# Last two output chunks merged into one, and DMA prices by row length in the planner of a hybrid decoder layer

## The chip, the core and the metric

The program runs on one core of one Trainium2 chip. The time is device microseconds of one execution; three executions of the kernel before gave 2155.23, 2158.32 and 2154.3 us, with a median of 2155.23 us. A separate, profiled execution took 2156.18 us, of which 2154.4 us is the span from its first to its last instruction. All durations below come from that execution.

## The reference, cut to what matters

One decoder layer is applied to 2048 prompt tokens and to 8 single decode tokens, all in float32 with width 1024. In the part that the change touches, the final RMSNorm divides each token's row by its root mean square and writes it out:

```python
x = x + jnp.concatenate([attn_out, conv_out, ssm_out], -1) @ w_out
hf = rmsnorm(x, norm_ffn_g)
x = x + (jax.nn.silu(hf @ w_ff_gate) * (hf @ w_ff_up)) @ w_ff_down
...
y_prompt = rmsnorm(xp, norm_final_g)     # (1, 2048, 1024)
y_sample = rmsnorm(xs, norm_final_g)     # (8, 1, 1024)
```

Before that lie the input projection, a sliding-window attention, a convolution and a state-space model (the first 650 us or so), and the output projection.

## The kernel before, in words

All 2056 tokens (2048 and then the 8) pass through one core. A float32 product is made of three passes of TensorE over a high and a low part of each operand, so each weight block that is loaded (`wraw`, `xraw`) is converted by ScalarE into its high part (`whl<-wraw`) and by VectorE or GpSimd into its low part before TensorE can use it. The first stages work in four quarters of 512 tokens. The gate and up products of the feed-forward part use a scheme with seven block products instead of eight: weight sums (`sw`) are formed on VectorE, kept in a scratch tensor (`sum`), and read back for later groups. The feed-forward part runs over three groups of tokens (g = 0, 1, 2; 688, 684 and 684 tokens), each group over 11 pairs of hidden blocks: gate and up products go to PSUM banks of the tag `mm` (three banks) or `tr` (two), the down products to `sc` (three), and VectorE adds the down products to an accumulator `xa`, which is eight tiles of features by tokens.

**The planner.** Nothing in the program is ordered by hand: class `Flow` (lines 45 to 174) simulates the kernel while it is being built. Each task is a generator that yields the engine it wants next, the buffers (tags) that it needs and the events it waits for. `Flow.run` (line 110) takes, again and again, the task that can begin first by the simulated clocks; among those of the same engine that begin within that engine's `SLACK` (TensorE 100 ns, VectorE 200, ScalarE 0, SyncE 50) it takes the one of the best priority. The order so found is each engine's instruction order on the chip, and each engine runs its queue in order: an instruction that waits holds everything behind it on that engine. All transfers are issued by SyncE through `Flow.dma` (line 163). It keeps one simulated clock, `DMA`, for all of them: a transfer begins when the one before it has ended, takes its bytes at 360 bytes per ns, or at 180 if a row is under 512 bytes, and counts as landed 2000 ns after its end. "Row" is the last dimension of the access, in bytes: 512 for a block of 128 columns of `w_ff_gate`, 2048 for `sum`, 4096 for `w_ff_down`, 1368 or 1376 for `hraw`.

Every instruction of the compute engines is emitted in one helper, so the profile puts them all on line 226; DMA issues are on line 164.

**The end of the kernel.** `final` (line 2187) handles one chunk of tokens. It waits for the down products of its tokens, takes two PSUM banks, transposes the eight `xa` tiles into them (four in each), has ScalarE square and sum each bank (`junkf`), VectorE add the two sums, ScalarE take the root (`stf`), VectorE invert it and scale the two halves by it and by the norm's weights (two instructions, 1.41 us in all), and SyncE write the chunk out. Group 2 has seven chunks: five of 128 tokens, one of the last 36 prompt tokens, and one of the 8 decode tokens. Their bank tags are written out in the tuple in `final`: `tr mm tr mm sc tr mm`. Chunk buffers for the result alternate between the tags `tx` and `whl`.

Of the kernel before, what the change touches and what calls it, by code (L numbers as in the profile page):

```python
# [19 lines left out]
T = 2048  # L20
NS = 8
# [31 lines left out]
class Flow:  # L53
# [89 lines left out]
    def rel(self, tag):  # L143
        self.free[tag].append(self.cur["fin"])
        self.free[tag].sort()
# [17 lines left out]
    def dma(self, out, in_):  # L163
        r = self.nc.sync.dma_start(out, in_)
        c = self.cur
        if c is not None:
            size, run = 4.0, 4.0 * min(in_.shape[-1], out.shape[-1])
            for d in in_.shape:
                size *= d
            start = max(self.clock["SP"], c["begin"])  # L170
            self.clock["SP"] = start + (650.0 if in_.shape[0] in (8, 64) else 475.0)
            self.clock["DMA"] = max(self.clock["DMA"], start + 1125.0) + size / 360.0 * (1.0 if run >= 512 else 2.0)
            c["fin"] = max(c["fin"], self.clock["DMA"] + 2000)
        return r

# [55 lines left out]
def hybrid_step(  # L231
# [13 lines left out]
    V, S = Engine(fl, "DVE", nc.vector), Engine(fl, "ACT", nc.scalar)  # L245
    G, E = Engine(fl, "POOL", nc.gpsimd), Engine(fl, "PE", nc.tensor)
    dma, rel = fl.dma, fl.rel
    ctx.enter_context(tc.manual_schedule())

# [89 lines left out]
    def load_unit(u, prio, pool=None, tag="whl", bufs=WB, after=0.0, keep=False, low="POOL"):  # L339
# [6 lines left out]
        def again():  # L346
            yield "SP", tag, kept_ev[u.key], *order
            taken.hit(0.0)
            hl = (pool or wpool).tile([P, 2, 1024], F32R, tag=tag, name=tag, bufs=bufs)
            dma(hl.bitcast(F32), kept[u.key])  # L350
            u.hl = hl.rearrange("p h (k c) -> p h k c", c=P)
            u.ready.hit(fl.now())
# [5 lines left out]
        def one():  # L358
            yield ("SP", "wraw", *([wturn] if wturn else []))
            wtaken.hit(0.0)  # L360
            raw = wpool.tile([P, 1024], F32, tag="wraw", name="wraw", bufs=2)
            u.load(raw)
            yield "ACT", tag, *order
            taken.hit(0.0)
            hl = (pool or wpool).tile([P, 2, 1024], F32R, tag=tag, name=tag, bufs=bufs)
            S.activation(hl[:, 0, :], raw, AF.Copy)
            yield low
            (G if low == "POOL" else V).tensor_tensor(hl[:, 1, :], raw, hl[:, 0, :].bitcast(F32), op=OP.subtract)
            rel("wraw")
            u.hl = hl.rearrange("p h (k c) -> p h k c", c=P)  # L370
            u.ready.hit(fl.now())
            if keep:
                yield "SP"
                dma(kept[u.key], hl.bitcast(F32))
                kept_ev[u.key].hit(fl.now())
# [1341 lines left out]
    G0 = [0, 688, 1372]  # L1717
# [39 lines left out]
    def tx_tile():  # L1757
        return bpool.tile([P, 1376], F32, tag="tx", name="tx", bufs=2)
# [179 lines left out]
    down_ev = {(g, j, a): Ev(KT // 2) for g in range(3) for j in range(2) for a in range(2)}  # L1938
    gu_ev = {g: Ev() for g in range(3)}
# [154 lines left out]
    b = "B22"  # L2094
# [85 lines left out]
    chunks = {}  # L2180
    for g in range(3):
        end = min(2 * GN[g], T - G0[g])
        chunks[g] = [(y_prompt[0, G0[g] + c:G0[g] + min(c + P, end), :], c, min(P, end - c)) for c in range(0, end, P)]
    chunks[2].append((y_sample[:, 0, :], T - G0[2], NS))
    fin_left = {g: len(chunks[g]) for g in range(3)}

    def final(g, i, dst, c0, n):

        bank = ("tr", "mm", "tr", "mm", "sc", "tr", "mm")[i] if g == 2 else "tr"
        st = fpool.tile([P, 4], F32, tag="stf", name="stf", bufs=4)  # L2190
        ev = Ev(2)
        for a in range(2):
            need = [down_ev[g, j, a] for j in range(2) if j * GN[g] < c0 + n and c0 < (j + 1) * GN[g]]
            if a == 0:
                yield ("PE", bank, bank, *need) if bank == "tr" else ("PE", bank, bank, gu_ev[2], *need)
                pts = [{"mm": ps_mm, "sc": ps_sc, "tr": ps_tr}[bank]() for _ in range(2)]
            else:
                yield ("PE", *need)
            pt = pts[a]
            for k in range(4):  # L2200
                E.transpose(pt[:n, k * P:(k + 1) * P], X[g, 4 * a + k][:, c0:c0 + n], ident)

            def square(a=a, pt=pt):
                yield "ACT"
                S.activation(junk[:n], pt[:n, :], AF.Square, accum_out=st[:n, a:a + 1])
                ev.hit(fl.now())
            fl.add(square(), 4)
        fin_left[g] -= 1
        if fin_left[g] == 0:
            for _ in range(KT):  # L2210
                rel("xa")
        tag = "whl" if g == 2 and i % 2 else "tx"
        yield ("DVE", ev, tag, gu_ev[2]) if tag == "whl" else ("DVE", ev, tag)
        if tag == "tx":
            y = tx_tile()[:, :D]
        else:
            y = wpool.tile([P, 2, D], F32R, tag="whl", name="y3", bufs=WB).bitcast(F32)[:, 0]
        V.tensor_tensor(st[:n, 0:1], st[:n, 0:1], st[:n, 1:2], op=OP.add)
        yield "ACT"
        S.activation(st[:n, 1:2], st[:n, 0:1], AF.Sqrt, scale=1.0 / D, bias=eps[:n])  # L2220
        yield "DVE"
        V.reciprocal(st[:n, 2:3], st[:n, 1:2])
        for a in range(2):
            cs = slice(a * 512, a * 512 + 512)
            V.scalar_tensor_tensor(y[:n, cs], pts[a][:n, :], st[:n, 2:3], gf_row[:n, cs], op0=OP.mult, op1=OP.mult)
            rel(bank)
        yield "SP"
        dma(dst, y[:n])
        rel(tag)

    for g in range(3):
        if g:
            fl.add(load_rs(g), -790 + g, after=t0)
            for kap in range(4):
                fl.add(prep_raw(g, kap), 100 + g, after=t0)
            for i, b in enumerate(USE):
                fl.add(prep_block(g, b), -790 + g + 0.1 * i, after=t0)
            fl.add(gate_up(g), 70 + g, after=t0)
        fl.add(down(g), 10 + g, after=t0)
        for m in range(KT):  # L2240
            fl.add(load_acc(g, m), -700 + 8 * g + m, after=t0)
        for i, (dst, c0, n) in enumerate(chunks[g]):
            fl.add(final(g, i, dst, c0, n), 5 + 0.1 * g + 0.01 * i, after=t0)
# [12 lines left out]
def _build(arrays):  # L2256
    import concourse.bacc as bacc

    nc = bacc.Bacc("TRN2", target_bir_lowering=False, num_devices=1, dynamic_dma_scratch_size=2048)
    args = [nc.dram_tensor(f"in_{n}", arrays[f"in_{n}"].shape, F32, kind="ExternalInput").ap() for n in _INS]  # L2260
    args += [nc.dram_tensor(f"out_{i}", s, F32, kind="ExternalOutput").ap() for i, s in enumerate(_OUTS)]
    with tile.TileContext(nc) as tc:
        hybrid_step(tc, *args)
    return nc
# [10 lines left out]
```

## Time and profile before

| | |
|---|---|
| median of three executions | 2155.23 us |
| the profiled execution | 2156.18 us, span 2154.4 us |
| TensorE busy | 2089.3 us (97%), 13326 matmuls |
| VectorE, ScalarE, GpSimd busy | 1539.8, 855.2, 253.6 us |
| DMA | 457.91 MB, mean 213 GB/s |
| granted TensorE clock, mean | 0.989 |

Busy times are those of one engine; idle time of an engine costs something only where it is the one that sets the end. The granted clock is a share of full speed, so 1.00 is TensorE's 2.4 GHz and a stretch at the lower level of 1.2 GHz reads 0.5. "DMA share" is the mean busy share of the core's 16 DMA engines as the profile counts it; values somewhat above 1 occur. In the lists of waits and in the timeline, `tile<-operands` names what an instruction writes and reads, and `[x <-E tile]` says how long the engine had been idle before it and which engine's write ended that.

### The profile page before, as it was taken

How to read it: one execution, taken by the hardware profiler on the slowest of the kernel's cores; microseconds unless marked ns; L12 is line 12 of the kernel's file. 1: busy time of each engine (PE TensorE's matmuls, PEld its weight loads, DVE VectorE, ACT ScalarE, POOL GpSimd, SP SyncE). 2: the span in 40 equal slices, each digit the busy share in tenths (PEclk: the TensorE clock that was granted, in tenths of full speed). 3: DMA queues.
4: the chain of work that ended last, by engine and by line, in shares of the span. 5: the costliest groups of instructions: out<-in, count | busy, mean ns of one | idle time of the engine just before them, and what ended most of it. 6: DMA issues, size and time to landing. Idle time of an engine off the chain costs nothing.

```text
span 2154.4 us, 35203 instructions
## 1 busy us (share of the span) xinstructions
PE 2089.3 (97%) x13326; PEld 1952.4 (91%) x13326; DVE 1539.8 (71%) x3060; ACT 855.2 (40%) x1684; POOL 253.6 (12%) x183
## 2 busy tenths in 40 slices
PE   8899999999999899999999999999999999999997
PEld 8677878776778899999999999999999999999997
DVE  5997889899865678787887765655656655555555
ACT  6216633777661434333333632222223622222223
POOL 3301110112211332222222000000000000000000
PEclk9999999999999999999999999999999999999999
DMA  8975766777879986655665786566557755545541
GB/s 265 297 234 178 237 190 197 222 224 234 241 243 374 311 283 205 212 199 183 213 227 175 231 269 212 166 198 212 182 166 257 231 178 177 176 156 161 181 152 53
DMA packets 351146, 457.91 MB, mean 213 GB/s; under 512 B 42501, under 2 KB 234320, under 8 KB 340736
## 3 DMA queue, kind: packets, MB, share of 16 engines
q1 hardware_dynamic: 350976, 455.66, 66.4%
q8 instruction: 105, 1.72, 0.3%
q14 instruction: 65, 0.53, 0.1%
HBM read 333.94 MB, written 122.32 MB: 212 GB/s over the span
## 4 chain that ended last, share of the span: by engine, by line
PE 59%; DMA 1%; DVE 1%; ACT 0%; issue 0%; DVEq 0%; SPq 0%; ACTq 0%
PE mm L226 32%; PE sc L226 22%; PE tr L226 5%; DMA tx<-hraw 1%; DMA xraw<-in_w_ff_gate 0%; DVE h L226 0%; ACT junkf L226 0%; ACT h L226 0%; DVE act L226 0%; DVE tx L226 0%; DVE y L226 0%; DVE xa L226 0%; DVE whl L226 0%; DVE sw L226 0%; DVE gs L226 0%
## 5 line engine op out<-in xcount | busy, mean ns | idle before, releaser
L226 PE MATMUL mm<-h,whl 128*128 128x342 f32 (+4 forms) x6576 | 1167.9, 332 | 13.7 <-DVE gs L226 4.6
L226 PEld LDWEIGHTS mm<-h,whl 128*128 128x128 f32 x6576 | 1042.5, 191 | 75.6 <-issue 11.5
L226 PE MATMUL sc<-act,whx 128*128 128x342 f32 (+1 forms) x3168 | 514.0, 319 | 2.1 <-ACT act L226 1.6
L226 PEld LDWEIGHTS sc<-act,whx 128*128 128x128 f32 x3168 | 499.5, 188 | 3.9 <-ACT act L226 1.9
L226 DVE TENSOR_TENSOR xa<-xa,sc 128x342 f32<-128x342 f32 (+1 forms) x528 | 264.3, 509 | 199.0 <-PE sc L226 198.0
L226 DVE SCALAR_TENSOR_TENSOR acc<-cu,taps,acc 128x512 f32<-128x512 f32 x240 | 180.1, 814 | 0.1
L226 ACT ACTIVATE whx<-wraw 128x1024 fp32r<-128x1024 f32 x66 | 66.5, 1053 | 239.6 <-PE sc L226 236.6
L226 POOL TENSOR_TENSOR whl<-sw,whl 128x512 fp32r<-128x512 f32 x88 | 123.2, 1410 | 321.5 <-ACT whl L226 314.7
L226 ACT ACTIVATE stg<-mm 128x342 f32<-128x342 f32 (+3 forms) x100 | 50.0, 502 | 247.5 <-PE mm L226 244.9
L226 PE MATMUL mm<-hb,whl 128*128 128x342 f32 (+1 forms) x792 | 136.0, 320 | 0.2 <-ACT gs L226 0.2
L226 PEld LDWEIGHTS mm<-hb,whl 128*128 128x128 f32 x792 | 126.3, 189 | 0.7 <-ACT gs L226 0.7
L226 PE MATMUL tr<-h,whl 128*128 128x342 f32 (+1 forms) x720 | 122.3, 319 | 0.0
L226 PEld LDWEIGHTS tr<-h,whl 128*128 128x128 f32 x720 | 114.5, 188 | 0.0
L226 ACT ACTIVATE whl<-wraw 128x512 fp32r<-128x512 f32 (+1 forms) x122 | 84.9, 697 | 59.5 <-PE mm L226 32.9
L226 DVE TENSOR_TENSOR whl<-wraw,whl 128x512 fp32r<-128x512 f32 x102 | 79.8, 784 | 24.3 <-ACT whl L226 23.8
L226 ACT ACTIVATE s<-s,sst 128x256 f32<-128x256 f32 (+1 forms) x192 | 89.1, 490 | 15.4 <-DVE sst L226 15.4
L226 DVE TENSOR_TENSOR whl<-xraw,whl 128x512 fp32r<-128x512 f32 x96 | 74.0, 774 | 29.5 <-ACT whl L226 29.3
L226 ACT ACTIVATE act<-gs 128x342 fp32r<-128x342 f32 (+1 forms) x99 | 48.1, 486 | 116.9 <-DVE gs L226 116.7
L226 ACT ACTIVATE whl<-xraw 128x512 fp32r<-128x512 f32 x96 | 60.1, 626 | 84.9 <-issue 59.1
L226 ACT ACT_TABLE_LOAD x68 | 87.2, 1283 | 12.6 <-PE mm L226 5.3
L226 DVE TENSOR_TENSOR whx<-wraw,whx 128x1024 fp32r<-128x1024 f32 x66 | 78.1, 1222 | 4.5 <-ACT whx L226 1.1
L226 ACT ACTIVATE whl<-sw 128x512 fp32r<-128x512 f32 x88 | 53.1, 625 | 69.3 <-PE mm L226 52.7
(237 smaller groups left out, 1944.5 us busy)
## 6 DMA issues: line engine op xcount, KB each, us to landing
whl<-sum SPq DMA_DIRECT2D x176, 512.0 KB
sum<-whl SPq DMA_DIRECT2D x88, 512.0 KB
wraw<-in_w_ff_down SPq DMA_DIRECT2D x66, 512.0 KB
whl<-hl_o SPq DMA_DIRECT2D x24, 1024.0 KB
wraw<-in_w_ff_up SPq DMA_DIRECT2D x44, 512.0 KB
xraw<-in_w_ff_gate SPq DMA_DIRECT2D x42, 512.0 KB
whl<-hl_q SPq DMA_DIRECT2D x12, 1024.0 KB
tx<-hraw SPq DMA_DIRECT2D x14, 684.0 KB
```

Source lines behind the costliest of these rows:

```text
L226: return call(*args, **kw)
```

## The change

Two edits. In `Flow.dma` the price per byte takes three values instead of two: 1/350 ns for rows of 2048 bytes and over, 1/300 for 512 to 2047, 1/180 below, as before. In the last group, the chunk of 36 prompt tokens and that of the 8 decode tokens become one chunk of 44 with two destinations; its two banks are one `mm` and one `sc`, and it waits for all down products of the group before its first transpose. All other chunks keep their banks.

```diff
-            self.clock["DMA"] = max(self.clock["DMA"], start + 1125.0) + size / 360.0 * (1.0 if run >= 512 else 2.0)
+            self.clock["DMA"] = max(self.clock["DMA"], start + 1125.0) + size * (1 / 350.0 if run >= 2048 else 1 / 300.0 if run >= 512 else 1 / 180.0)
...
-    chunks[2].append((y_sample[:, 0, :], T - G0[2], NS))
+    dst, c, n = chunks[2].pop()
+    chunks[2].append(((dst, y_sample[:, 0, :]), c, n + NS))
...
-        bank = ("tr", "mm", "tr", "mm", "sc", "tr", "mm")[i] if g == 2 else "tr"
+        b0, b1 = ((("tr", "tr"), ("mm", "mm"), ("tr", "tr"), ("mm", "mm"), ("sc", "sc"), ("mm", "sc"))[i] if g == 2
+                  else ("tr", "tr"))
...
-                yield ("PE", bank, bank, *need) if bank == "tr" else ("PE", bank, bank, gu_ev[2], *need)
-                pts = [{"mm": ps_mm, "sc": ps_sc, "tr": ps_tr}[bank]() for _ in range(2)]
+                if b1 != b0:
+                    need = [down_ev[g, j, x] for j in range(2) for x in range(2)]
+                yield ("PE", b0, b1, *need) if b0 == "tr" else ("PE", b0, b1, gu_ev[2], *need)
+                pts = [{"mm": ps_mm, "sc": ps_sc, "tr": ps_tr}[b]() for b in (b0, b1)]
...
-            rel(bank)
+            rel((b0, b1)[a])
         yield "SP"
-        dma(dst, y[:n])
+        if isinstance(dst, tuple):
+            dma(dst[0], y[:n - NS])
+            dma(dst[1], y[n - NS:n])
+        else:
+            dma(dst, y[:n])
```

## Rows read from the trace of the kernel before

**Rows 1.** The page: busy time of TensorE.

```profile
PE 2089.3 (97%) x13326; PEld 1952.4 (91%) x13326; DVE 1539.8 (71%) x3060; ACT 855.2 (40%) x1684; POOL 253.6 (12%) x183
```

**Rows 2.** Stretches: length, PE, PEld, DVE, ACT, POOL busy, clock, DMA share, GB/s.

```profile
0.00:162.00 162.00, 140.85 (x886) 119.55 (x886) 136.76 (x400) 57.52 (x93) 33.90 (x25) 0.94 0.86 265
162.00:648.00 486.00, 466.07 (x2997) 364.53 (x2998) 415.59 (x980) 297.77 (x670) 79.06 (x57) 0.99 0.71 219
648.00:864.00 216.00, 204.74 (x1296) 195.62 (x1295) 146.20 (x211) 77.46 (x137) 58.43 (x41) 0.97 0.87 293
864.00:2106.00 1242.00, 1241.36 (x7921) 1238.99 (x7920) 812.08 (x1412) 405.64 (x742) 82.26 (x60) 1.00 0.61 195
2106.00:2155.00 49.00, 36.27 (x233) 33.76 (x231) 29.14 (x62) 16.82 (x43) 0.00 (x0) 0.91 0.15 58
```

**Rows 3.** What TensorE waited for: us in total, times, longest.

```profile
PE tr L226 <- DVE s L226: 6.8, 2, 6.4
...
PE mm L226 <- DVE gs L226: 4.6, 1, 4.6
...
PE tr L226 <- DMA xo<-in_x_prompt: 2.3, 2, 2.0
```

**Rows 4.** Timeline at 56 us: start, duration, engine, operation.

```profile
55.81 1.06 ACT L226 ACTIVATE whl<-wraw 128x1024 fp32r<-128x1024 f32 x1 [3.27 <-DMA wraw<-in_w_in]
...
56.77 1.03 ACT L226 ACTIVATE stg<-mm 128x256 f32<-128x256 f32 x2
...
57.41 4.87 PE L226 MATMUL mm<-h,whl 128*128 128x256 f32 x26 [3.02 <-ACT stg L226]
```

**Rows 5.** Timeline from 752 to 764 us.

```profile
752.39 1.74 SPq L164 DMA_DIRECT2D xraw<-in_w_ff_gate  x2
...
761.33 0.69 DVE L226 TENSOR_TENSOR sw<-xraw 128x512 f32<-128x512 f32 x1 [1.63 <-DMA xraw<-in_w_ff_gate]
...
762.72 0.51 DVE L226 TENSOR_TENSOR gs<-mm,gs 128x344 f32<-128x344 f32 x1
...
763.29 0.94 PE L226 MATMUL mm<-h,whl 128*128 128x344 f32 x2 [4.56 <-DVE gs L226]
```

**Rows 6.** Two stretches of 2 us with transfers of one row length.

```profile
757.00:759.00 2.00, 1.73 (x11) 1.44 (x10) 2.00 (x2) 0.73 (x2) 2.00 (x2) 1.00 1.10 313
...
793.00:795.00 2.00, 2.00 (x15) 2.00 (x14) 1.97 (x5) 0.08 (x1) 0.00 (x0) 1.00 1.05 406
```

**Rows 7.** Timeline of SyncE: issues that precede the second of these.

```profile
787.69 4.38 SPq L164 DMA_DIRECT2D sum<-whl  x4
```

**Rows 8.** The page: the main DMA queue's packets, MB, share of 16 engines.

```profile
q1 hardware_dynamic: 350976, 455.66, 66.4%
```

**Rows 9.** Timeline of the end, from 2139 us.

```profile
2140.18 0.60 PE L226 MATMUL sc<-ident,xa 128*128 128x128 f32 x4
...
2142.03 0.65 ACT L226 ACTIVATE stf<-stf,eps 128x1 f32<-128x1 f32 x3
...
2143.44 1.86 PE L226 MATMUL tr<-ident,xa 128*36 128x128 f32 x8 [2.66 <-DVE tx L226]
...
2144.49 0.59 ACT L226 ACTIVATE junkf<-tr 36x512 bf16<-36x512 f32 x1 [1.81 <-PE tr L226]
...
2145.57 1.41 DVE L226 SCALAR_TENSOR_TENSOR tx<-sc,stf,gf_row 128x512 f32<-128x512 f32 x2
...
2147.59 0.28 ACT L226 ACTIVATE stf<-stf,eps 36x1 f32<-36x1 f32 x1
...
2148.24 1.40 DVE L226 SCALAR_TENSOR_TENSOR y<-tr,stf,gf_row 36x512 f32<-36x512 f32 x2 [0.19 <-DVE stf L226]
...
2149.67 0.32 SPq L164 DMA_DIRECT2D out<-y  x1
...
2150.37 1.40 DVE L226 SCALAR_TENSOR_TENSOR tx<-mm,stf,gf_row 8x512 f32<-8x512 f32 x2
2151.80 0.29 SPq L164 DMA_DIRECT2D out<-tx  x1
```

## Prediction

> **What bounds the kernel now.** I read the page first: TensorE is busy 2089.3 of the span's 2154.4 us [rows 1], so all idle time of the engine that sets the end is 65.1 us. The stretches say where it lies [rows 2]: 21.2 us (162 - 140.85) in the first 162 us, 19.9 in the next 486, 11.3 between 648 and 864, 0.6 in the 1242 us of the feed-forward part, and 12.1 from 2106 to the end at 2154.4. The clock column of the same rows is 0.94, 0.99 and 0.97 in the first three, 1.00 in the fourth. The reader should see two things: for 58% of the span nothing but matmuls counts and there is nothing to win, and the change can act only before 864 us (through the order of the queues) and after 2139 us (through the merged chunk).
>
> Next, the list of TensorE's waits names single stalls: 6.4, 4.6 and 2.0 us are the longest of three kinds [rows 3]. I followed two of the stalls in the timeline, to see whether a transfer stands behind them though the list names ScalarE or VectorE. It does. At 57.41 us TensorE had been idle 3.02 us for a PSUM bank that two `stg<-mm` copies were to empty; these stood in ScalarE's queue behind a weight conversion that had itself waited 3.27 us for its weights to land [rows 4]. At 763.29 it had been idle 4.56 us for a `gs<-mm` addition which stood in VectorE's queue behind two `sw` sums; the first of these had waited 1.63 us for a pair of gate blocks (512-byte rows) issued at 752.39 [rows 5]. Both are the planner's misjudgement: it put the consumer of a transfer ahead of work that was ready, since it reckoned the transfer earlier than it came.
>
> **The change part by part: the merged chunk.** In the trace [rows 9], chunk 4 (the last of 128 tokens) ends its transposes at 2140.78 (2140.18 + 0.60) and its scaling at 2146.98 (2145.57 + 1.41). The chunk of 36 wants two `tr` banks, which chunk 2 holds: it waits 2.66 us and transposes from 2143.44, 1.86 us long; its scaling begins at 2148.24. The chunk of 8 follows with sum, root and inverse, scaling from 2150.37, issue at 2151.80; the span ends 2.60 us after that issue.
>
> Removed: eight transposes, two squares, and on the path the last chunk's step from scaling to scaling, 2150.37 - 2148.24 = 2.13 us. Moved: the merged chunk's banks (one `mm`, one `sc`) are free without chunk 2, so its transposes can run at 2140.8 to 2142.7. ScalarE still squares and takes roots for chunks 2 to 4 until 2142.68 (2142.03 + 0.65); the squares of the merged chunk then take what they took for the 36 tokens, 0.59 us each, which with the read of the sum I count as 0.8, to about 2144.3, and the root 0.28. All this lies beside VectorE's scaling of chunks 3 and 4, which hides it. VectorE goes on with the merged chunk right after chunk 4: 2146.98 plus a short inverse and gaps, about 2147.3 instead of 2148.24, which is 0.9 us. Scaling took 1.40 us for 36 tokens and 1.40 for 8, so 44 cost no more. Added: a second output transfer in SyncE's queue. One issue took 0.32 us; with its gap I count 0.4 on the path, since nothing else stands behind it. Sum: 2.13 + 0.9 - 0.4 = 2.6 us less.
>
> Bounds: if the root and the inverse come only after chunk 4's scaling, the scaling begins near 2147.9 and 2.0 us are left; if the second issue costs nothing, 3.0. If the cover is gone altogether, because the planner gives the merged chunk a bank only when chunk 4 leaves its own at 2146.98, then transposes to first square (1.05), two squares (1.6) and root to scaling (0.65) put the scaling at 2150.3, and with the second issue the end comes 0.3 us later than before. The wait for all down products costs nothing: chunk 4's second half waits for the same last additions.
>
> **The change part by part: the prices.** No instruction is added or removed; the simulated landing of each transfer moves. 512 KB with 512-byte rows went for 1.46 us (524288 / 360) and goes for 1.75; 512 KB with rows of 2 KB or more 1.46 to 1.50; an `hraw` block of 684 KB 1.95 to 2.33. In a line of four weight loads the last lands about 1.2 us later in the planner, and every task that waits for it may change places with one that it stood before.
>
> Are the new prices truer? In 757 to 759 us, when the pair of [rows 5] was moving, 313 GB/s at a share of 1.10 are 285 GB/s for busy engines; in 793 to 795, with `sum` rows of 2 KB issued before [rows 7], 406 / 1.05 = 387 [rows 6]. Over the whole span the main queue moved 455.66 MB in 66.4% of 2154.4 us, 319 GB/s [rows 8]. So 360 was 26% too fast for 512-byte rows, and 300 is 5% too fast; 350 for long rows is further from an undisturbed 387 than 360 was, but the mean of 319 says that few are undisturbed.
>
> The Trainium skill, "DMA: Bandwidth & Descriptors", Specifications, gives 512 bytes as the least transfer for line rate. That speaks against pricing such rows apart: by it the old price was right and the new one defers their consumers for nothing. The trace disagrees, 285 against 387, so I give this little weight; what it would do is the second rival below.
>
> What the truer prices are worth in time: in the feed-forward part nothing, since TensorE stands idle 0.6 us in 1242 at a DMA share of 0.61 [rows 2], and weights that come a pair ahead hide shifts of about a microsecond; if that cover went, a pair of gate blocks would show, 1.05 MB or 3.7 us at 285 GB/s, at each of the two changes of group. Before 864 us the gain is bounded by the stalls in which an in-order queue sat on a late transfer: 3.02 + 4.56 + 2.3 for the `xo` rows = 9.9 us [rows 3 to 5]. The loss is bounded by new stalls of the longest sizes seen, 6.4 + 4.6 = 11 us. Between -9.9 and +11 I take 0: a shift of 0.3 us per transfer swaps two tasks only where the planner had them that close, while ScalarE's queue in [rows 4] was 3.27 us out. Most of the misjudged places stay, and the swaps that come fall on either side.
>
> **Rivals.** (1) Late transfers leave the queues. The simulated pair of gate blocks lands after the `gs<-mm` addition becomes ready, so the addition goes first, and likewise the copies at 56.77. For it: in [rows 5] the addition is one of a few candidates, and 1.63 us of waiting and 1.4 us of sums stand before it. Against: the shift is small. One to three stalls of 3 to 4.6 us go, 5 us in the middle: 2155.2 - 2.6 - 5 = 2147.6.
>
> (2) Consumers deferred (slower). With all landings reckoned later, weight conversions go behind other work on ScalarE and VectorE, the weights are ready late, and TensorE stalls on `whl` where it did not. The place is 0 to 162 and 648 to 864 us, where the DMA share is 0.86 and 0.87 and VectorE is busy 84% and 68% [rows 2]. Price: two stalls of the longest kinds, 11 us, so 2155.2 - 2.6 + 11 = 2163.6; it decides from 7 us on, since 2.6 + 4.3 must be made up first. Against: these stretches already hold waits in which work came too early, not too late.
>
> (3) A little of (2): one stall of 4.6 us, which eats the merged chunk's gain: 2157.2. That the prices change no order that matters is part of my forecast.
>
> **How the numbers follow.** The profiled execution took 2156.18 us, 1.78 more than its span and 0.95 more than the median. Against itself: 2156.2 - 2.6 = 2153.6; against the median, 2155.23 - 2.6 = 2152.6 us. This is the forecast, with a chance of 0.43 and a range of its own from 2150.8 to 2154.5 (order worth less than 2 us either way). Rival 1 has 0.35, rival 3 0.10, rival 2 0.12. A measurement of this kernel can tell 0.2%, 4.3 us, from no change. Faster than 2150.9 comes from rival 1, 0.35; slower than 2159.5 from rival 2, 0.12; the rest, 0.53, is no change. The range that leaves out 0.1 on each side runs from 2146 (two or three stalls gone) to 2159.
>
> **What would show it.** Right: the last two of the seven output issues, 2.1 us apart before, within half a microsecond; merged transposes before 2141.5 on this time line; the stretch from TensorE's last down product to the end shorter by 2 to 3 us; TensorE's idle time from 864 to 2106 still under 2 us; idle time before 864 within 2 us of 52.3. Wrong: merged transposes that wait for a scaling, a new wait of TensorE on `whl` or `h` of over 3 us, the stalls near 57 and 763 us gone, or idle time at the changes of group. A change of more than 7 us would mean that the order, and not the chunk, decides.

## The result and the profile after

The changed kernel takes 2191.56 us (median of four runs, 2187.62 to 2195.64), against 2156.59 us for the kernel before in the same series (2154.3 to 2158.32): a ratio of 1.0159, 95% interval 1.0146 to 1.0171. By the medians it is 35 us slower, by the ratio 34. The forecast was 2152.6 us in a range of 2146 to 2159, so sign and size were both wrong. The profiled execution took 2190.36 us, with a span of 2188.3 us.

The first fence is the page's line of busy times, which answers to [rows 1]; the second is the same stretches as [rows 2], with the same columns and the last one drawn out to the new end.

```profile
PE 2093.8 (96%) x13318; PEld 1954.8 (89%) x13318; DVE 1529.8 (70%) x3053; ACT 844.5 (39%) x1672; POOL 255.1 (12%) x183
```

```profile
0.00:162.00 162.00, 136.85 (x871) 115.87 (x872) 133.56 (x399) 57.79 (x94) 34.94 (x25) 0.92 0.83 255
162.00:648.00 486.00, 452.55 (x2902) 355.81 (x2901) 389.95 (x958) 269.36 (x635) 71.24 (x50) 0.96 0.66 205
648.00:864.00 216.00, 196.26 (x1198) 178.98 (x1197) 141.45 (x188) 85.27 (x144) 58.99 (x42) 0.97 0.89 303
864.00:2106.00 1242.00, 1239.66 (x7908) 1236.87 (x7907) 818.60 (x1419) 409.09 (x746) 89.93 (x66) 1.00 0.61 196
2106.00:2188.30 82.30, 68.50 (x447) 67.28 (x446) 46.22 (x93) 23.05 (x54) 0.00 (x0) 0.94 0.30 102
```

TensorE's idle time grew from 65.1 to 94.5 us (2188.3 - 2093.8), which is 29.4 of the 33.9 us by which the span grew; the other 4.5 us are longer busy time, at a clock column of 0.92 and 0.96 in the first two stretches against 0.94 and 0.99. By stretch the idle time before 864 us is now 25.2, 33.4 and 19.7 us, against 21.2, 19.9 and 11.3: 26 us more. The feed-forward part stays nearly free of it (2.3 us). So the time was lost where the prediction said that the change could act, but not in the size it allowed.

The list of TensorE's waits of the changed kernel answers to [rows 3]:

```profile
PE mm L226 <- ACT h L226: 11.3, 2, 8.5
PE tr L226 <- DVE s L226: 7.4, 3, 6.4
PE tr L226 <- DVE stg L226: 6.9, 1, 6.9
PE tr L226 <- DMA xo<-in_x_prompt: 6.0, 4, 2.9
PE tr L226 <- DVE acc L226: 5.7, 2, 5.1
PE tr L226 <- DVE GT L226: 5.3, 1, 5.3
```

The 6.4 us on `s` stood there before. New are single stalls of 8.5, 6.9, 5.3 and 5.1 us. Two of them, on `acc` and `stg`, lie close together, and they are the thread to pull. A finer cut shows how concentrated the loss is: the stretch from 540 to 648 us had 1.3 us of idle time in the kernel before and has 16.5 now, at a clock of 0.92 instead of 1.00. First before, then after (columns as in [rows 2]); the second row of each is the end of the way into the feed-forward part, 4.6 us idle before and 15.9 after:

```profile
540.00:648.00 108.00, 106.72 (x554) 79.80 (x553) 83.04 (x209) 67.58 (x175) 19.75 (x14) 1.00 0.80 247
756.00:864.00 108.00, 103.38 (x640) 102.69 (x639) 84.84 (x130) 43.66 (x79) 31.11 (x22) 0.97 0.74 246
```

```profile
540.00:648.00 108.00, 91.54 (x479) 71.05 (x478) 87.57 (x208) 52.61 (x138) 13.41 (x12) 0.92 0.66 208
756.00:864.00 108.00, 92.10 (x563) 89.67 (x562) 77.28 (x106) 51.10 (x84) 32.88 (x23) 0.94 0.79 265
```

**What happened at 540 us.** The array `cu` is the convolution's input; VectorE writes it as the last step of a projection unit, in two products, one for each token tile. The convolution of the last quarter (`acc<-cu,taps`, two scalings and then 60 multiply-adds of 0.7 us) can start only when its last unit is there. The timelines around that point, first VectorE before, then VectorE and TensorE after (start, duration, engine, operation):

```profile
442.70 0.42 DVE L226 TENSOR_TENSOR cu<-mm,stg 128x256 f32<-128x256 f32 x1
445.37 0.43 DVE L226 TENSOR_TENSOR cu<-mm,stg 128x264 f32<-128x264 f32 x1 [0.21 <-PE mm L226]
446.12 1.00 DVE L226 TENSOR_SCALAR acc<-cu,taps,fv 128x512 f32<-128x512 f32 x2
...
472.15 0.68 DVE L226 TENSOR_TENSOR x<-mm,x 128x512 f32<-128x512 f32 x1
```

```profile
466.08 0.68 DVE L226 TENSOR_TENSOR x<-mm,x 128x512 f32<-128x512 f32 x1
...
566.55 0.66 DVE L226 TENSOR_TENSOR x<-mm,x 128x512 f32<-128x512 f32 x1
...
574.31 0.41 DVE L226 TENSOR_TENSOR cu<-mm,stg 128x256 f32<-128x256 f32 x1
581.36 0.43 DVE L226 TENSOR_TENSOR cu<-mm,stg 128x264 f32<-128x264 f32 x1 [0.64 <-PE mm L226]
581.71 0.99 DVE L226 TENSOR_SCALAR acc<-cu,taps,fv 128x512 f32<-128x512 f32 x2
...
587.27 1.13 PE L226 MATMUL tr<-ident,stg 120*128 120x120 f32 x4 [5.09 <-DVE acc L226]
...
595.30 0.62 PE L226 MATMUL tr<-ident,cu 128*38 128x128 f32 x2 [6.90 <-DVE stg L226]
...
605.52 1.94 PE L226 MATMUL tr<-ident,xo 128*128 128x128 f32 x8 [2.90 <-DMA xo<-in_x_prompt]
...
608.37 0.68 DVE L226 TENSOR_TENSOR x<-mm,x 128x512 f32<-128x512 f32 x1
```

Before, the last unit was multiplied at 440 to 445 us, 27 us ahead of the first output projection (`x<-mm`, 472.15). After, the output projections start first, at 466.08, and the unit comes 115 us later. In the code the projections of the input (`w_stream`, line 1306) have priority 50, the output projections (`out_stream`, line 2086) 45 and the attention blocks 10 to 40; the lower number goes first. As long as the last unit is multiplied before the output projections are ready, its priority decides nothing. If it is not, it loses every choice on TensorE until they run out of input. They do: part of their input is the convolution, which waits for the unit. Then TensorE has nothing to put beside the 60 multiply-adds: 5.09, 6.90 and 2.90 us of idle time (the last of them ended by a transfer of `xo`), and no `x<-mm` between 567 and 608 us. I call this the starved unit. From 540 to 648 us it cost 15.2 us. Part of that is work done sooner: with output projections going ahead of the unit, TensorE is idle for 5.0 us from 440 to 540 us, where it was for 8.7 before. Over both stretches the idle time grew from 10.0 to 21.4 us, so 11.5 us is the net cost. First before, then after:

```profile
440.00:540.00 100.00, 91.33 (x534) 70.32 (x535) 96.34 (x281) 76.19 (x212) 21.14 (x14) 1.00 0.78 233
```

```profile
440.00:540.00 100.00, 95.01 (x582) 74.83 (x580) 68.10 (x260) 71.41 (x208) 23.05 (x13) 0.98 0.78 226
```

The stalls that [rows 4] and [rows 5] show are, in the profile after:

```profile
57.27 7.10 PE L226 MATMUL mm<-h,whl 128*128 128x256 f32 x53 [2.53 <-ACT stg L226]
...
770.50 0.42 PE L226 MATMUL mm<-h,whl 128*128 128x344 f32 x1 [2.89 <-ACT h L226]
...
782.54 1.35 ACT L226 ACTIVATE h<-tx 128x1376 fp32r<-128x1376 f32 x1 [5.23 <-DMA tx<-hraw]
783.94 0.66 PE L226 MATMUL mm<-h,whl 128*128 128x344 f32 x1 [8.45 <-ACT h L226]
```

The first stayed, 2.53 us against 3.02. The second is gone as such (the longest wait on `gs` there is 1.7 us), but in its place TensorE waits 2.89 and 8.45 us for `h`, the latter behind a read of `hraw` for which ScalarE stood idle 5.23 us. The main queue moved the same bytes in nearly the same time as in [rows 8]: 65.1% of 2188.3 is 1425 us, 66.4% of 2154.4 was 1431.

```profile
q1 hardware_dynamic: 350976, 455.66, 65.1%
```

The end of the kernel, which answers to [rows 9]; the first fence is the last addition to `xa` before, which [rows 9] do not show:

```profile
2139.01 0.51 DVE L226 TENSOR_TENSOR xa<-xa,sc 128x342 f32<-128x342 f32 x1 [0.39 <-PE sc L226]
```

```profile
2173.83 0.51 DVE L226 TENSOR_TENSOR xa<-xa,sc 128x342 f32<-128x342 f32 x1 [0.39 <-PE sc L226]
...
2175.44 0.60 PE L226 MATMUL mm<-ident,xa 128*44 128x128 f32 x4
...
2175.87 0.60 PE L226 MATMUL sc<-ident,xa 128*44 128x128 f32 x4
...
2177.70 0.59 ACT L226 ACTIVATE junkf<-sc 44x512 bf16<-44x512 f32 x1
...
2178.29 0.84 ACT L226 ACTIVATE stf<-stf,eps 128x1 f32<-128x1 f32 x4
...
2178.80 1.41 DVE L226 SCALAR_TENSOR_TENSOR tx<-tr,stf,gf_row 128x512 f32<-128x512 f32 x2
...
2183.49 0.74 DVE L226 SCALAR_TENSOR_TENSOR y<-mm,stf,gf_row 44x512 f32<-44x512 f32 x1 [0.19 <-issue]
2184.16 0.73 DVE L226 SCALAR_TENSOR_TENSOR y<-sc,stf,gf_row 44x512 f32<-44x512 f32 x1
2184.92 0.67 SPq L164 DMA_DIRECT2D out<-y  x2
```

From the last addition to `xa` to the end of the span it takes 14.42 us (2188.25 - 2173.83), where it took 15.40 before (2154.41 - 2139.01). The merged chunk is transposed right behind chunk 4 and scaled right behind it, as predicted, but it saves 1.0 us and not 2.6. ScalarE takes the squares of the merged chunk first and then all four roots, at 2178.29, 4.46 us after the last addition instead of 3.02 (2142.03 - 2139.01). And from the first of the last two issues to the end it takes 3.33 us (2188.25 - 2184.92), where from the last issue before it took 2.61 (2154.41 - 2151.80).

### The profile page after: what moved, and what is told of

It reads as the page before. It is cut to its first block, busy times and chain, and to the rows that moved or that the text cites. A ratio compares the mean times of both kernels' runs of the same rounds, so it can differ in the third digit from the quotient of the medians.

```text
span 2188.3 us, 35188 instructions
## 1 busy us (share of the span) xinstructions
PE 2093.8 (96%) x13318; PEld 1954.8 (89%) x13318; DVE 1529.8 (70%) x3053; ACT 844.5 (39%) x1672; POOL 255.1 (12%) x183
## 3 DMA queue, kind: packets, MB, share of 16 engines
q1 hardware_dynamic: 350976, 455.66, 65.1%
## 5 line engine op out<-in xcount | busy, mean ns | idle before, releaser
L226 PE MATMUL mm<-h,whl 128*128 128x342 f32 (+4 forms) x6576 | 1167.7, 332 | 22.2 <-ACT h L226 11.3
L226 PEld LDWEIGHTS mm<-h,whl 128*128 128x128 f32 x6576 | 1042.5, 190 | 85.8 <-ACT h L226 12.1
L226 DVE SCALAR_TENSOR_TENSOR acc<-cu,taps,acc 128x512 f32<-128x512 f32 x240 | 168.6, 767 | 0.0
L226 DVE TENSOR_TENSOR whl<-xraw,whl 128x512 fp32r<-128x512 f32 x96 | 78.9, 826 | 26.5 <-ACT whl L226 25.7
L226 ACT ACT_TABLE_LOAD x58 | 74.4, 1283 | 18.8 <-PE mm L226 7.8
```

What stands on the lines that cost most here:

```text
L226: return call(*args, **kw)
```

## The experiments

The time of each is given as a ratio to the kernel before on the same chip, since that one's median itself was 2158.3 to 2159.7 us in the four series. The theory to test was the starved unit. Against it stood two rivals: that long rows or short rows were now priced worse (the direction of the price matters), and that 360 was a point to which everything else had been fitted, so that any other order costs a per cent.

**The merged chunk alone.** The new chunks, and of the diff only this left out:

```diff
-            self.clock["DMA"] = ... + size * (1 / 350.0 if run >= 2048 else 1 / 300.0 if run >= 512 else 1 / 180.0)
+            self.clock["DMA"] = ... + size / 360.0 * (1.0 if run >= 512 else 2.0)
```

> The merged last chunk alone, with the old transfer prices. All instructions before the last ones of group 2 keep their order. In the changed kernel the end from the last addition to xa to the end of the span took 14.47 us against 15.39 before, since ScalarE squared the merged chunk before it took the roots of chunks 2 to 4. If the chunk is as good as free of the loss, this kernel is 0.9 us faster than before (ratio 0.9996, not distinguishable from 1). If the chunk itself costs the 34 us (for example through its wait for all down products), it is as slow as the changed kernel, 2190 us.

Measured: ratio 1.0007 (0.9998 to 1.0016), 14.86 us from the last addition to the end in the profiled execution. The chunk is not the loss, and its gain is below what can be told.

**The merged chunk, its squares behind the roots.**

```diff
-            fl.add(square(), 4)
+            fl.add(square(), 4 if b0 == b1 else 6)
```

> As merge_only, and the squares of the merged chunk get a worse priority than the roots of the other chunks. If the roots that came 1.44 us late are what ate the forecast gain of 2.6 us, the end after the last addition to xa is now 13.0 to 13.4 us long (15.39 before, 14.47 changed): 2.0 to 2.4 us faster than before, ratio 0.9990. If something else ate it, it stays near 14.5 us.

Measured: ratio 1.0000 (0.9988 to 1.0011), end part 13.78 us, 1.6 shorter than before but longer than the 13.0 to 13.4 expected. Of the missing 1.0 us, 0.4 is the root of the merged chunk, which ScalarE now takes only after chunk 4's scaling (the case behind the prediction's bound of 2.0). The other 0.6 is the second issue: from the first of the two to the end of the span it takes 3.63 us (2155.60 - 2151.97), 1.0 more than from the last issue before.

```profile
2149.88 0.29 ACT L226 ACTIVATE stf<-stf,eps 44x1 f32<-44x1 f32 x1 [3.25 <-DVE stf L226]
...
2151.97 0.67 SPq L164 DMA_DIRECT2D out<-y  x2
```

In the five kernels with the merged chunk this last piece is 3.33 to 3.78 us long, in the nine without it 2.61 to 2.94.

**The changed kernel, input projections ahead of the output projections.** At the old price this edit changes no instruction's place, and in the changed kernel none ahead of the last unit.

```diff
-    fl.add(w_stream(plan), 50)
+    fl.add(w_stream(plan), 44)
```

> The changed kernel, with the priority of the input projections raised from 50 to 44, above the output projections (45). Theory A (a starved unit): with the new prices the last projection unit of quarter 3 is not done when the output projections begin, then loses every choice against them and comes at 574 us instead of 443, and the convolution of quarter 3 starts at 582 instead of 446; here that convolution should start before 490 us and some 20 of the 35 us come back: 2165 to 2175 us. Theory B (all consumers deferred a little, by prices that are too long): the raised priority moves little, 2185 to 2195 us.

Measured: ratio 1.0073 (1.0053 to 1.0092), 2175.65 us, just above the 2165 to 2175 that the theory allowed. The last `cu` comes at 486.05 instead of 581.36, the convolution starts at 491.65, and the idle time from 540 to 648 us is back at 1.8:

```profile
540.00:648.00 108.00, 106.23 (x555) 82.43 (x554) 93.23 (x226) 61.43 (x152) 21.51 (x16) 1.00 0.75 241
```

So the starved unit holds, and moving it gives back about half of the loss (1.59% to 0.73%). Not all of that is the unit's own stretch: in the profiled executions the idle time falls by 18.5 us, 11.6 of them between 440 and 648 us and 4.3 between 648 and 864.

**The price on the other side.** The chunks of before, and

```diff
-            ... + size / 360.0 * (1.0 if run >= 512 else 2.0)
+            ... + size / 365.0 * (1.0 if run >= 512 else 2.0)
```

> The kernel before with one price still, but 365 bytes per ns instead of 360 (182.5 below 512 bytes): transfers are reckoned 1.4% shorter, the other way from the change. Theory B: shorter prices defer nothing, so it is as fast as before or faster, at most 5 us slower. Theory C (the order at 360 is a short one, and almost any other price gives a longer one): 20 to 45 us slower, 2176 to 2200 us, with the last projection unit of quarter 3 again after 550 us.

Measured: ratio 1.0242 (1.0226 to 1.0257), 2210.93 us, more than either theory allowed. The unit is late here too (last `cu` at 553.0), with 15.1 us idle from 540 to 648. A price error in the other direction does the same harm, so the direction is not the cause.

**New prices late only** (for transfers that start after 640 us on the planner's clock; here and in the next three the chunks of before).

```diff
-            ... + size / 360.0 * (1.0 if run >= 512 else 2.0)
+            ... + size * ((1 / 350.0 if run >= 2048 else 1 / 300.0 if run >= 512 else 1 / 180.0) if start > 640000.0
+                          else (1 / 360.0 if run >= 512 else 1 / 180.0))
```

> The kernel before with the new prices only for transfers that the planner starts after its 640th us (the last quarter's output projection, the way into the feed-forward part, and that part). The projections of quarter 3 keep their place, so theory A (the starved unit) leaves nothing of its 19 us here. If the rest of the loss, 16 us in new_44, arises at the way into the feed-forward part, this kernel is 8 to 16 us slower than before (2166 to 2174 us); if that rest lies in the stages before, it is within 4 us of before.

Measured: ratio 1.0033 (1.0021 to 1.0045), 7.7 us by the medians and so just under the 8 to 16 expected for a loss at the entry, the unit in its old place. The longest wait of TensorE between 648 and 864 us:

```profile
PE mm L226 <- DVE x L226: 7.5, 3, 5.1
```

A second loss, some 7 us, exists without the starved unit: at the entry of the feed-forward part, where idle time is 20.0 instead of 11.3 us.

**New prices in the middle only** (from 60 to 640 us; the lines show the difference to late_only).

```diff
-                          if start > 640000.0
+                          if 60000.0 <= start <= 640000.0
```

> The kernel before with the new prices only for transfers that the planner starts between its 60th and 640th us. Theory A: the starvation is made here, so the last projection unit of quarter 3 comes after 550 us and the kernel is 20 to 35 us slower than before (2178 to 2193 us). If the loss were made at the start or after 640 us, it is under 10 us slower.

Measured: ratio 1.0144 (1.0122 to 1.0166), as expected. Nearly the whole loss, with the last `cu` at 582.8 and 17.0 us idle from 540 to 648.

**Only the long rows repriced** (350 from 2048 bytes on, 360 for 512 to 2047; 0.04 us for a transfer of 512 KB).

```diff
-            ... + size / 360.0 * (1.0 if run >= 512 else 2.0)
+            ... + size * (1 / 350.0 if run >= 2048 else 1 / 360.0 if run >= 512 else 1 / 180.0)
```

> The kernel before with one of the two new prices: 350 for rows of 2048 bytes and over, 360 still for 512 to 2047. The step that reading the trace speaks for (512-byte rows at 285 GB/s) is left out; what is left is a shift of 0.04 us per 512 KB. Theory C with A: this is enough to lose the race, the last unit of quarter 3 comes after 550 us, 15 to 35 us slower than before (2173 to 2193 us). Theory B: a shift so small costs under 5 us.

Measured: ratio 1.0156 (1.0128 to 1.0184), the same loss, with the last `cu` at 589.4. The 512-byte rows, whose price moved most, are not needed for it.

**365 with the input projections at 44:** the edits of price_365 and new_44 together.

> price_365 with the priority of the input projections at 44. Theory A holds for it too: the last unit of quarter 3 came at 465 to 553 us there, so some 20 of its 52 us come back, 2183 to 2195 us. If the raised priority helps only with the new prices, it stays above 2203 us.

Measured: ratio 1.0189 (1.017 to 1.0209). The unit came at 469.8 and the idle time from 540 to 648 fell to 1.6 us, but less came back than expected, and 12.1 us of idle time turned up between 864 and 1300 us, where the kernel before has 0.3.

**The changed kernel at 44 with the old prices after 640 us, and the middle prices at 44.** These were to close the account: new_44 less the late loss, and mid_span_only less the unit. The first is new_44 with

```diff
-            ... + size * (1 / 350.0 if run >= 2048 else 1 / 300.0 if run >= 512 else 1 / 180.0)
+            ... + size * ((1 / 350.0 if run >= 2048 else 1 / 300.0 if run >= 512 else 1 / 180.0) if start <= 640000.0
+                          else (1 / 360.0 if run >= 512 else 1 / 180.0))
```

and the second is mid_span_only with the priority edit of new_44 (and the chunks of before).

> As new_44 (the changed kernel with the input projections' priority at 44), but with the new prices only for transfers that the planner starts before 640 us; those after it keep the old price. new_44 stood 16 to 17 us over the kernel before. If the losses add, the 7.7 us that late_only cost go: 2166 to 2170 us, with the last projection unit multiplied near 468 to 486 us and TensorE's first feed-forward product before 765 us. If the late loss was not a loss of the late prices but of what arrives late from the earlier stage, the time stays at 2173 or more.

> As mid_span_only (new prices only between the planner's 60th and 640th us, the old chunks, ratio 1.0144), with the input projections' priority at 44. If the last unit's lost race is all that the middle prices cost, the 31 us over the kernel before go nearly all: 2158 to 2165 us, last unit before 490 us, first feed-forward product before 757 us. If other changes of order in the middle cost as well, 2168 to 2175 us, with the unit early all the same and the first feed-forward product at 760 us or later.

Measured: 1.0183 (1.016 to 1.0206) and 1.0157 (1.013 to 1.0183). Both are misses. The unit is early in both (last `cu` at 485.8 and 485.5) and its stretch is mended, but the time is that of the changed kernel. Against mid_span_only, mid_44 has 15.9 us less idle time from 540 to 648 us, and 10.8 more from 864 to 1300, 6.0 more before 540 and 1.9 more from 648 to 864: the feed-forward part lost its cover. Against new_44, early_44 has 11.7 us more from 864 to 1300 and 4.6 more from 648 to 864. For mid_44 the two stretches, its waits from 864 to 1300 us, and one of these in the timeline:

```profile
540.00:648.00 108.00, 106.87 (x559) 83.02 (x558) 92.82 (x226) 61.94 (x152) 21.24 (x16) 1.00 0.75 243
756.00:864.00 108.00, 95.37 (x582) 93.98 (x581) 83.14 (x116) 48.73 (x87) 33.91 (x23) 0.97 0.75 246
864.00:1300.00 436.00, 423.78 (x2674) 421.55 (x2673) 332.73 (x530) 168.30 (x307) 89.60 (x64) 0.99 0.61 199
```

```profile
PE mm L226 <- DVE gs L226: 11.5, 6, 2.2
```

```profile
1011.67 1.35 DVE L226 TENSOR_TENSOR whl<-xraw,whl 128x512 fp32r<-128x512 f32 x1 [0.79 <-ACT whl L226]
...
1012.95 0.68 DVE L226 TENSOR_TENSOR sw<-xraw 128x512 f32<-128x512 f32 x1
1013.55 0.50 DVE L226 TENSOR_TENSOR gs<-mm,stg 128x344 f32<-128x344 f32 x1
...
1014.11 2.16 PE L226 MATMUL mm<-h,whl 128*128 128x344 f32 x12 [1.91 <-DVE gs L226]
```

Six times, about 1.9 us each, TensorE waits for a PSUM bank that a `gs` addition must empty, and the addition stands on VectorE behind the making of the next weights. That is the pattern of [rows 5], now repeated from pair to pair. It stands in mid_44, early_44 and price_365_44, whose units are early, and in none of the four kernels with a late unit, so the late unit does not make it.

**The price one unit to either side**, 361 and 359, the chunks of before. Both change the order of instructions on every engine, and both leave the unit ahead of the output projections.

> The kernel before with the one price at 361 instead of 360 (0.3%), old chunks. In its order the last projection unit stands 65 VectorE instructions ahead of the first output projection, as in the kernel before (56), so by the starved-unit theory TensorE's idle time from 540 to 648 us is under 3 us (15 to 17 where the unit came late). What the time does is the second question. If the losses beside the starved unit are only what a new order brings by chance, on either side, the time is between 2150 and 2170 us. If 360 is a point to which everything else was fitted, so that any other order costs a per cent or more, it is 2175 to 2200 us in spite of the early unit.

> The same on the other side, 359: the unit stands 85 VectorE instructions ahead of the first output projection. The same two ways: idle from 540 to 648 us under 3 us in either; 2150 to 2170 us if the rest is chance on either side, 2175 to 2200 us if any other order costs a per cent or more.

Measured: 1.0016 (1.0003 to 1.0029) and 1.002 (1.0006 to 1.0034); first 361, then 359:

```profile
540.00:648.00 108.00, 106.85 (x547) 81.15 (x546) 81.57 (x197) 59.23 (x147) 17.37 (x13) 1.00 0.81 255
```

```profile
540.00:648.00 108.00, 107.99 (x569) 81.56 (x568) 86.73 (x217) 66.85 (x178) 18.23 (x14) 1.00 0.79 244
```

Two other orders cost 0.2% each, so it is not true that any order but that of 360 costs a per cent. Where the unit keeps its place, these two new orders cost 3 to 4 us. In 361 the idle time from 648 to 864 us grew by 5.8 us; 359 has no more idle time up to 1300 us than the kernel before.

All kernels together, from their windows (idle time is length less TensorE's busy time, in us):

| kernel | ratio | last `cu` at | idle 0-540 | 540-648 | 648-864 | 864-1300 |
|---|---|---|---|---|---|---|
| before | 1 | 445.4 | 39.8 | 1.3 | 11.3 | 0.3 |
| merge_only | 1.0007 | 448.9 | 36.7 | 2.0 | 12.0 | 0.8 |
| merge_roots | 1.0000 | 445.9 | 40.4 | 1.8 | 11.4 | 0.7 |
| price_361 | 1.0016 | 438.7 | 38.9 | 1.2 | 17.1 | 1.2 |
| price_359 | 1.0020 | 446.6 | 39.7 | 0.0 | 11.5 | 0.4 |
| late_only | 1.0033 | 446.1 | 40.4 | 1.0 | 20.0 | 0.2 |
| new_44 | 1.0073 | 486.1 | 44.7 | 1.8 | 15.4 | 0.3 |
| mid_44 | 1.0157 | 485.5 | 45.5 | 1.1 | 18.8 | 12.2 |
| early_44 | 1.0183 | 485.8 | 42.6 | 2.1 | 20.0 | 12.0 |
| price_365_44 | 1.0189 | 469.8 | 50.0 | 1.6 | 17.8 | 12.1 |
| mid_span_only | 1.0144 | 582.8 | 39.5 | 17.0 | 16.9 | 1.4 |
| long_only | 1.0156 | 589.4 | 44.4 | 16.1 | 14.3 | 0.5 |
| after | 1.0159 | 581.4 | 42.2 | 16.5 | 19.7 | 0.4 |
| price_365 | 1.0242 | 553.0 | 44.9 | 15.1 | 26.1 | 3.1 |

The column 540-648 splits the kernels without exception: 0 to 2.1 us in the ten whose unit is done before 490 us, 15.1 to 17.0 in the four in which it comes after 550. From 440 us on, so that work done sooner counts too, it is 7.6 to 10.7 us in the ten and 20.1 to 24.7 in the four.

## Why the prediction was wrong

**The prices: the step that failed** is "Between -9.9 and +11 I take 0: a shift of 0.3 us per transfer swaps two tasks only where the planner had them that close ... Most of the misjudged places stay, and the swaps that come fall on either side." This term, put at 0 with 11 us as its worst, came to 26 us of idle time before 864 us. The first half may be true of one choice. But each choice moves every clock after it, and the step weighed swaps as if each cost only its own stall. One swap, the last projection unit against the first output projection, put a unit 115 us behind an output projection that it had led by 27, and with it the 60 multiply-adds that feed everything behind. A shift of 0.04 us per transfer was enough for it (long_only). The swap is shown as the cause of the idle time from 540 to 648 us: that time stands in every kernel in which the swap occurs and in none in which it doesn't, and one changed priority takes 13.5 to 15.9 us of it away in three pairs of kernels. Net of the work done sooner, it is 11.5 of the 29.4 us of new idle time. This is shown by moving a late unit forward; no run makes the unit late at the old prices.

**The bound of 11 us** was worked out from the longest stalls of the trace before. Stalls that a trace shows are those of its own order; they say nothing of the stalls of another one. What the code showed, and I did not use, was a priority of 50 below one of 45 and a lead of 27 us from the unit's last `cu` to the first output projection, and behind them a stretch, 540 to 648 us, whose 1.3 us of idle time gave no sign of what it had to lose.

**Rival 2** (slower, 0.12) was right in sign and not in mechanism. It placed the loss at 0 to 162 and 648 to 864 us, where 4.0 and 8.5 us were indeed added, but the largest part lies between these, and none of TensorE's waits there is on `whl`. **Rival 1** named one stall rightly: that of [rows 5] went, and others of 2.89 and 8.45 us on `h` took its place. That truer prices removed it is not shown: at 361, 359 and 365 the longest wait on `gs` between 690 and 864 us is 2.4 to 2.6 us too. No time was gained: the order around it changed as well.

**Whether the prices are truer** did not decide it. long_only leaves the 512-byte rows at their old price and lost as much as the change did. The Trainium skill, "DMA: Bandwidth & Descriptors", Specifications, gives 512 bytes as the least transfer for line rate. The prediction's rows stand against that, 285 against 387 GB/s, and no run here measures it by itself. That prices nearer to the measured rates lose 34 us, and prices at 365 lose 52 (2.42% of 2156), is the same point: what was gained or lost was an order.

**The merged chunk:** its mechanism was right and two terms of the sum were mis-sized. "ScalarE still squares and takes roots for chunks 2 to 4 until 2142.68 (2142.03 + 0.65); the squares of the merged chunk then" took the order of [rows 9] for given. The squares went ahead of the roots, which set VectorE's first scaling back by 1.44 us. Counted from the last addition to `xa`, the merged chunk's scaling began 0.43 us later than that of the 36 tokens had (9.66 against 9.23 us), where 0.9 us earlier was forecast. And the second issue was counted as 0.4 us and cost 0.72 (3.33 - 2.61), though the two issues took only 0.67 us together. So 2.13 - 0.43 - 0.72 = 1.0 us was left of the 2.6. merge_roots puts the squares behind and has 1.6.

**The signs named beforehand** did their work: idle time before 864 us is 78.3 us against "within 2 us of 52.3", `h` is waited for over 3 us, the end is shorter by 1.0 us against "2 to 3", the feed-forward part has 2.3 us of idle time against "under 2", and by "a change of more than 7 us would mean that the order, and not the chunk, decides" it is the order.

**What stays open:** the rest. Of the 26 us before 864 us, 14.5 lie outside 440 to 648: 4.0 before 162, 2.0 from there to 440, and 8.5 from 648 to 864, the entry of the feed-forward part. In the profile after, the largest part of the last is the wait on `h`; mid_span_only and price_365, with a late unit too, wait 6.7 and 13.1 us for it there, the kernels with an early unit at most 3.9, but long_only, whose unit is late, not at all. late_only shows a loss of that kind from the late prices alone, but early_44 has 20.0 us idle from 648 to 864 without them, so the cause cannot be put down to one range of prices. Nor do the losses add: with the unit early, new_44 gained 0.86% and mid_44 nothing, since the waits on `gs` and idle time before 540 us came instead. What sends three of the four kernels at 44 into that pattern was not found.

## What to carry to other kernels

Where a planner writes the order, a changed cost is a new order, and its price cannot be summed from stalls of the old trace: give it a wide range, mostly on the slow side where the old order is already a good one (all seven other price rules run here were slower, by 0.2 to 2.4%). Before changing the planner, look in the trace for pairs of streams that compete for one engine, where the one with the worse priority feeds the other, and measure the lead by which it comes first; here 27 us of lead hid a wrong priority. A mended race is judged by its own stretch first, because the total holds everything else that the new order did.

## What the runs showed of the hardware

The same instructions in the same order up to the last 20 us do not run at the same clock each time. In the first 162 us, for the kernel before, merge_only and merge_roots, TensorE is idle for 21.2, 21.5 and 21.8 us, but the granted clock is 0.94, 0.92 and 0.95; over the whole run TensorE is busy 2089.3, 2098.4 and 2087.8 us, and the spans are 2154.4, 2164.4 and 2155.6 us. The idle time over the whole run is 65.1, 66.0 and 67.8 us. A profile of one execution can thus be 10 us longer than another of nearly the same program, 9 us of it busy time, without any new wait, which is why the end part of these kernels was compared from the last addition to `xa` on. In the changed kernel the one long stall on `GT` stands in a stretch of low clock: from 104 to 128 us TensorE is busy 18.71 us at 0.73, against 22.45 at 0.83 before.
